# Moving three adjacent groups per partition with two large DMAs, in a group-mean subtraction that is limited by memory traffic

## The chip, the core and the metric

The kernel runs on one core of a Trainium2 chip; the chip's other cores are not used. The metric is device time in microseconds for one execution. One execution was also recorded by the hardware profiler; its page and its trace are what is read here. The engines that matter are DVE (the vector engine, which does all the arithmetic), SP and ACT (whose queues issue the DMAs), and the core's 16 DMA engines, which move data between the chip's memory (HBM) and the core's on-chip memory of 128 partitions.

## The reference

```python
def setup_inputs():
    B, S, D = 8, 4096, 2112
    return {"x": np.random.randn(B, S, D).astype(np.float32)}

def reference(x):
    B, S, D = x.shape
    stride = 4
    x_r = x.reshape(B, S // stride, stride, D)
    pooled = x_r.mean(axis=2)
    upsampled = np.repeat(pooled, stride, axis=1)
    return (x - upsampled).astype(np.float32)
```

Four consecutive rows of 2112 floats form a group. The mean of the group's rows is subtracted from each of them. Input and output are 276.8 MB each. There are 8 x 4096 / 4 = 8192 groups, and a group is one contiguous run of 4 x 2112 x 4 = 33,792 bytes in memory.

## The kernel before

The tensor is seen as 8192 groups of W = 8448 floats, `xg` on the input side and `og` on the output side. One loop takes 128 groups at a time, one to a partition, so it runs 64 times. Below, "a group" in the sense of time means one such pass: 128 partitions with one group each, 4.3 MB in and 4.3 MB out.

In each pass, SP's queue loads the 128 groups into a buffer of the pool `io` (L39), one DMA of 128 rows of 33,792 bytes. The pool has six such buffers. DVE then adds the first two rows into the tile `s` (L43), adds the other two rows to it (L45, twice), and with a single instruction over all four rows (L46) multiplies the sum by -1/4 and adds it to the data in place. ACT's queue stores the buffer (L54), again with a DMA of 128 rows of 33,792 bytes.

There is no schedule written by hand. Each queue works through its own list in program order: SP holds only loads, ACT only stores, DVE only arithmetic. The framework inserts the waits: DVE waits for a load, a store waits for DVE, and a load into a buffer waits until the store that emptied that buffer, six passes earlier, has landed. The tile `s` has one buffer, which only DVE writes and reads. SP and ACT feed the same 16 DMA engines, through one queue each (q1 and q10 on the page).

Of the kernel before, what the change touches and what calls it, by code (L numbers as in the profile page):

```python
# [1 line left out]

# [4 lines left out]

STRIDE = 4
IO_BUFS = 6  # L10


@with_exitstack
def kernel(
    ctx: ExitStack,
    tc: tile.TileContext,
    x: bass.AP,
    out: bass.AP,
):

    nc = tc.nc
    B, S, D = x.shape
    P = nc.NUM_PARTITIONS
    assert S % STRIDE == 0
    G = (B * S) // STRIDE
    W = STRIDE * D

    xg = x.rearrange("b (g f) d -> (b g) (f d)", f=STRIDE)  # L30
    og = out.rearrange("b (g f) d -> (b g) (f d)", f=STRIDE)

    io_pool = ctx.enter_context(tc.tile_pool(name="io", bufs=IO_BUFS))
    sum_pool = ctx.enter_context(tc.tile_pool(name="sum", bufs=1))

    for g0 in range(0, G, P):
        gsz = min(P, G - g0)
        x_tile = io_pool.tile([P, W], mybir.dt.float32)
        nc.sync.dma_start(out=x_tile[:gsz], in_=xg[g0:g0 + gsz])  # L39

        rows = x_tile[:gsz].rearrange("p (f d) -> p f d", f=STRIDE)
        s = sum_pool.tile([P, D], mybir.dt.float32)
        nc.vector.tensor_add(out=s[:gsz], in0=rows[:, 0, :], in1=rows[:, 1, :])  # L43
        for f in range(2, STRIDE):
            nc.vector.tensor_add(out=s[:gsz], in0=s[:gsz], in1=rows[:, f, :])  # L45
        nc.vector.scalar_tensor_tensor(  # L46
            out=rows,
            in0=s[:gsz, None, :].to_broadcast([gsz, STRIDE, D]),
            scalar=-1.0 / STRIDE,
            in1=rows,  # L50
            op0=mybir.AluOpType.mult,
            op1=mybir.AluOpType.add,
        )
        nc.scalar.dma_start(out=og[g0:g0 + gsz], in_=x_tile[:gsz])  # L54


# [1 line left out]
_INS = ['x']  # L58
_OUTS = [((8, 4096, 2112), 'float32')]


# [23 lines left out]
```

## Time and profile before

| | |
|---|---|
| median of 7 runs | 1286.52 us (1286.4 to 1286.9) |
| the profiled execution, its own time | 1286.53 us |
| its span in the profile | 1284.8 us |
| DVE busy | 1026.1 us, 256 instructions |
| bytes moved | 553.70 MB, mean 431 GB/s over the span |
| one load: issue to landing, median | 59.6 us, 64 DMAs of 4224 KB |
| one store: issue to landing, median | 43.8 us, 64 DMAs of 4224 KB |
| one L46 on DVE | 8958 ns, 64 times |
| one L43 or L45 on DVE | 2358 ns, 64 and 128 times |

The time of an execution is a little longer than the span, which runs from the first to the last recorded event of the program. "Issue to landing" is the time from the queue's issue of a DMA to the completion of its last byte; it contains the time that the DMA spends behind others in the queue. A packet is one piece of a DMA as a DMA engine handles it. The share of a queue on the page is the time that its packets took, over the 16 engines' span, and counts only time on the engines.

### The profile page before, as it was taken

To read this page: it belongs to the slowest core of one execution; us is meant where nothing else is said; L and a number is where in the kernel's file an instruction comes from. 1 tells how busy PE (TensorE), PEld (TensorE's weight loads), DVE (VectorE), ACT (ScalarE), POOL (GpSimd) and SP (SyncE) were. 2 spreads that over 40 slices of the span, in tenths; PEclk is the share of its full clock that TensorE was granted. 3 is DMA by queue.
4 is the path that set the end of the run, shared out by engine and by line. 5 is a ranking of instruction groups with operands and counts; after the bars stand their busy time and mean duration, and the time that the engine had idled before them with its cause. 6 is when DMAs were issued, how large, how long until landed. Compare 5 with 4: busy or idle time off the path is not lost.

```text
span 1284.8 us, 674 instructions
## 1 busy us (share of the span) xinstructions
DVE 1026.1 (80%) x256; POOL 0.2 (0%) x4
## 2 busy tenths in 40 slices
DVE  5998778787787877878778787787887878778784
POOL 0000000000000000000000000000000000000000
DMA  9999999999999999999999999999999999999998
GB/s 404 421 438 437 431 428 437 430 437 430 437 430 435 432 436 431 430 436 437 431 429 438 436 428 432 438 433 430 432 437 432 432 431 437 429 433 433 438 429 382
DMA packets 18437, 553.70 MB, mean 431 GB/s; under 512 B 2048, under 2 KB 2048, under 8 KB 2048
## 3 DMA queue, kind: packets, MB, share of 16 engines
q1 hardware_dynamic: 9216, 276.83, 50.0%
q10 hardware_dynamic: 9216, 276.83, 49.9%
q14 instruction: 5, 0.04, 0.0%
HBM read 276.82 MB, written 276.82 MB: 431 GB/s over the span
## 4 chain that ended last, share of the span: by engine, by line
DVE 80%; another core or an unknown queue 17%; DMA 1%; issue 1%; DVEq 0%
DVE x_tile L46 45%; DVE s L45 24%; DVE s L43 12%; DMA x_tile<-in_x_dram 1%; DVEq L43 0%
## 5 line engine op out<-in xcount | busy, mean ns | idle before, releaser
L46 DVE SCALAR_TENSOR_TENSOR x_tile<-s,x_tile 128x8448 f32<-128x8448 f32 x64 | 573.3, 8958 | 2.2
L43 DVE TENSOR_TENSOR s<-x_tile 128x2112 f32<-128x2112 f32 x64 | 150.9, 2358 | 237.5 <-DMA x_tile<-in_x_dram 237.4
L45 DVE TENSOR_TENSOR s<-s,x_tile 128x2112 f32<-128x2112 f32 x128 | 301.8, 2358 | 4.4
L69 POOL MEMSET const-bfloat16-1.0<- 128x1 bf16 x1 | 0.1, 101 | 0.0
L69 POOL MEMSET const-uint8-127<- 128x1 uint8 x1 | 0.1, 101 | 0.0
L69 POOL MEMSET const-float32-0.0<- 128x1 f32 x1 | 0.1, 98 | 0.2 <-issue 0.2
L69 POOL MEMSET const-float32-1.0<- 128x1 f32 x1 | 0.1, 98 | 0.0
## 6 DMA issues: line engine op xcount, KB each, us to landing
x_tile<-in_x_dram SPq DMA_DIRECT2D x64, 4224.0 KB, 59.6
out_dram<-x_tile ACTq DMA_DIRECT2D x64, 4224.0 KB, 43.8
```

What stands on the lines that cost most here:

```text
L43: nc.vector.tensor_add(out=s[:gsz], in0=rows[:, 0, :], in1=rows[:, 1, :])
L45: nc.vector.tensor_add(out=s[:gsz], in0=s[:gsz], in1=rows[:, f, :])
L46: nc.vector.scalar_tensor_tensor(out=rows, in0=s[:gsz, None, :].to_broadcast([gsz, STRIDE, D]), scalar=-1.0 / STRIDE, in1=rows, op0=mybir. ...
L69: nc = _bacc.Bacc("TRN2", target_bir_lowering=False, num_devices=1)
```

## The change

The pool of six buffers becomes one tile, `ring`, of six slots of W floats in each partition: the same size in total. The 64 passes are grouped into blocks: three blocks of one group, nineteen blocks of three groups, four blocks of one group. A block of one is handled as before. In a block of three, each partition owns three adjacent groups of the tensor, a contiguous run of 101,376 bytes in memory and in the ring. This run is moved by two DMAs of 50,688 bytes a partition in each direction. A half therefore holds one and a half groups. DVE still works group by group, with the same four instructions on the same shapes; the middle group of a block needs both halves. The first half is stored after the block's second group, the second half after its third. The three single blocks take slots 0 to 2, the blocks of three take slots 3 to 5 and 0 to 2 in turn, ending in slots 3 to 5, and the last four single blocks take slots 0 to 3.

```diff
-IO_BUFS = 6
+RING = 6
+SUPER = 3
+HEAD = 3
+TAIL = 4
...
-    io_pool = ctx.enter_context(tc.tile_pool(name="io", bufs=IO_BUFS))
+    n = G // P
+    n_super = (n - HEAD - TAIL) // SUPER
+    blocks = [1] * HEAD + [SUPER] * n_super
+    blocks += [1] * (n - sum(blocks))
+
+    ring_pool = ctx.enter_context(tc.tile_pool(name="ring", bufs=1))
     sum_pool = ctx.enter_context(tc.tile_pool(name="sum", bufs=1))
+    ring = ring_pool.tile([P, RING * W], mybir.dt.float32)
 
-    for g0 in range(0, G, P):
-        gsz = min(P, G - g0)
-        x_tile = io_pool.tile([P, W], mybir.dt.float32)
-        nc.sync.dma_start(out=x_tile[:gsz], in_=xg[g0:g0 + gsz])
-
-        rows = x_tile[:gsz].rearrange("p (f d) -> p f d", f=STRIDE)
+    def reduce_group(c0: int):
+        rows = ring[:, c0:c0 + W].rearrange("p (f d) -> p f d", f=STRIDE)
         s = sum_pool.tile([P, D], mybir.dt.float32)
...
-        nc.scalar.dma_start(out=og[g0:g0 + gsz], in_=x_tile[:gsz])
+
+    g0 = 0
+    slot = 0
+    for k in blocks:
+        assert slot + k <= RING
+        src = xg[g0:g0 + k * P].rearrange("(p j) w -> p (j w)", j=k)
+        dst = og[g0:g0 + k * P].rearrange("(p j) w -> p (j w)", j=k)
+        c0 = slot * W
+        parts = 1 if k == 1 else 2
+        step = k * W // parts
+        for h in range(parts):
+            nc.sync.dma_start(
+                out=ring[:, c0 + h * step:c0 + (h + 1) * step],
+                in_=src[:, h * step:(h + 1) * step],
+            )
+        stored = 0
+        for j in range(k):
+            reduce_group(c0 + j * W)
+            while stored < parts and (stored + 1) * step <= (j + 1) * W:
+                nc.scalar.dma_start(
+                    out=dst[:, stored * step:(stored + 1) * step],
+                    in_=ring[:, c0 + stored * step:c0 + (stored + 1) * step],
+                )
+                stored += 1
+        g0 += k * P
+        slot = (slot + k) % RING
```

More of the change, by code (lines that the diff above doesn't have):

```diff
@@ L25 @@
     P = nc.NUM_PARTITIONS
-    assert S % STRIDE == 0
+    W = STRIDE * D
     G = (B * S) // STRIDE
-    W = STRIDE * D
+    assert S % STRIDE == 0 and G % P == 0 and (SUPER * W) % 2 == 0
     xg = x.rearrange("b (g f) d -> (b g) (f d)", f=STRIDE)
     og = out.rearrange("b (g f) d -> (b g) (f d)", f=STRIDE)
-    io_pool = ctx.enter_context(tc.tile_pool(name="io", bufs=IO_BUFS))
-    sum_pool = ctx.enter_context(tc.tile_pool(name="sum", bufs=1))
-    for g0 in range(0, G, P):
-        gsz = min(P, G - g0)
-        x_tile = io_pool.tile([P, W], mybir.dt.float32)
-        nc.sync.dma_start(out=x_tile[:gsz], in_=xg[g0:g0 + gsz])
-        rows = x_tile[:gsz].rearrange("p (f d) -> p f d", f=STRIDE)
+    n = G // P
[3 more added lines that the diff above has]
+    ring_pool = ctx.enter_context(tc.tile_pool(name="ring", bufs=1))
+    sum_pool = ctx.enter_context(tc.tile_pool(name="sum", bufs=1))
+    ring = ring_pool.tile([P, RING * W], mybir.dt.float32)
+    def reduce_group(c0: int):
+        rows = ring[:, c0:c0 + W].rearrange("p (f d) -> p f d", f=STRIDE)
         s = sum_pool.tile([P, D], mybir.dt.float32)
-        nc.vector.tensor_add(out=s[:gsz], in0=rows[:, 0, :], in1=rows[:, 1, :])
+        nc.vector.tensor_add(out=s, in0=rows[:, 0, :], in1=rows[:, 1, :])
         for f in range(2, STRIDE):
-            nc.vector.tensor_add(out=s[:gsz], in0=s[:gsz], in1=rows[:, f, :])
+            nc.vector.tensor_add(out=s, in0=s, in1=rows[:, f, :])
         nc.vector.scalar_tensor_tensor(
             out=rows,
-            in0=s[:gsz, None, :].to_broadcast([gsz, STRIDE, D]),
+            in0=s[:, None, :].to_broadcast([P, STRIDE, D]),
             scalar=-1.0 / STRIDE,
```

## The prediction

> **What bounds the kernel now.** I read the page first, then the busy time by stretch, then the waits, then the timeline of single groups. From the page:
>
> ```profile
> span 1284.8 us, 674 instructions
> DVE 1026.1 (80%) x256; POOL 0.2 (0%) x4
> DMA packets 18437, 553.70 MB, mean 431 GB/s; under 512 B 2048, under 2 KB 2048, under 8 KB 2048
> q1 hardware_dynamic: 9216, 276.83, 50.0%
> q10 hardware_dynamic: 9216, 276.83, 49.9%
> DVE 80%; another core or an unknown queue 17%; DMA 1%; issue 1%; DVEq 0%
> ```
>
> The chain of waits puts 80% on DVE, and that misleads. The two DMA queues together hold the 16 engines for 99.9% of the span. The chain names DVE because it follows each store back to the instruction that released it, while the time is set by how fast the queues drain. Of 18,437 packets, 2048 are completion writes (128 DMAs by 16 engines), a handful are instruction fetches, and 16,384 carry data: 128 a DMA, so one packet for each partition, 33,792 bytes long.
>
> The stretches, with columns of stretch, length, DVE busy, POOL busy, clock, DMA share, GB/s:
>
> ```profile
> 0.00:30.00 30.00, 16.53 (x5) 0.20 (x4) 1.00 0.96 406
> 110.00:1180.00 1070.00, 855.66 (x216) 0.00 (x0) 1.00 1.00 433
> 1255.00:1285.00 30.00, 15.18 (x4) 0.00 (x0) 1.00 0.87 375
> ```
>
> From 110 to 1180 us the DMA engines have no idle time. Only the first and last 30 us have any: 4% and 13%. No reordering of work can win in the middle; only fewer engine-nanoseconds can.
>
> The waits and two groups of the timeline:
>
> ```profile
> DVE s L43 <- DMA x_tile<-in_x_dram: 237.4, 59, 13.3
> SPq L39 <- DMA out_dram<-x_tile: 1158.3, 58, 40.7
> 154.09 2.36 DVE L43 TENSOR_TENSOR s<-x_tile 128x2112 f32<-128x2112 f32 x1 [3.84 <-DMA x_tile<-in_x_dram]
> 174.06 2.36 DVE L43 TENSOR_TENSOR s<-x_tile 128x2112 f32<-128x2112 f32 x1 [3.83 <-DMA x_tile<-in_x_dram]
> ```
>
> DVE starves 3.83 us a group, and the load queue waits for stores to free buffers. One group takes 174.06 - 154.09 = 19.97 us. In that time each engine moves 8 load packets, 8 store packets and 2 completion writes: 19.97 / 16 = 1.248 us a packet.
>
> **The change part by part.** Bytes, the DVE instructions (64 groups of 3 x 2.358 + 8.958 = 16.03 us, 16.17 with the gaps) and the first three and last four groups stay. What moves:
>
> *Fewer packets.* 57 of 64 groups become 19 blocks of three. Each engine did 57 x 16 = 912 data packets for them and now does 19 blocks x 2 DMAs x 2 directions x 8 = 608, of 50,688 bytes: 304 fewer on each engine. Their bytes are not saved, only what a packet costs beyond its bytes. The profile of before has one size of data packet, so this must be bounded. The trace's single packet records show 1251 ns for 16,114 of the 16,384 data packets, 307 to 309 ns for 8192-byte instruction fetches, and 9 ns for the 4-byte completion writes. Lower end: 0, if time is proportional to bytes. Upper end: 9 ns, since a packet with almost no bytes takes no longer than that. Between: the two larger sizes give (1251 - 307) / (33,792 - 8192) = 0.0369 ns a byte and 307 - 8192 x 0.0369 = 4.9 ns left over. I take 4.9, because it comes from large packets. 304 x 4.9 ns = 1.49 us; ends 0 and 2.74 us. A loss is not excluded by these rows; it is priced in the rivals.
>
> The Trainium skill ("DMA: Bandwidth & Descriptors", "Why small descriptors are slow") gives a packet about 3 cycles of fixed cost on the engine's inner bus; with the page's 850 MHz that is an estimate of 3.5 ns, and 304 of them would be 1.1 us. Its section "Anatomy of one DMA" instead gives every DMA about 2 us of fixed cost, and 38 fewer DMAs would then be worth 76 us; the stretch at DMA share 1.00 says that this fixed part lies under other transfers, so the measurement decides against counting it.
>
> *Fewer DMAs.* Each direction goes from 64 to 7 + 38 = 45. That takes 38 completion writes off every engine: 38 x 9 ns = 0.34 us, on the same saturated engines. Issue time on SP and ACT (0.33 us a DMA) lies beside transfers that are tens of microseconds deep, so it is worth nothing; without that cover 19 fewer issues a queue would be 6 us.
>
> *Coarser waits.* A first half covers one and a half groups, and its store can leave only when the second group is done. A half-load waits for the store of the same half two blocks earlier; behind it on SP is only the next load, and ACT has only stores behind its wait. Does the engine queue run dry? A buffer comes round every 6 x 19.97 = 119.8 us. Before: load 20.0 at shared rate, DVE 16.2, store 20.0, and two handovers of 1.4 us (first issue at 0.73, first packet at 1.74, so 1.0; last completion of the first load at 12.95, DVE at 13.33, so 0.4): 59 us, slack 61. After: a half is 6.49 MB; at the shared 433 GB/s its load and its store take 2 x 6.49 / 433 = 30.0 us each. The first half is held for two groups, 32.3 us, or 30.0 + 16.2 = 46.2 if its partner lands a whole half-load later: 95 to 109 us, slack 11 to 25. The second half is held for 32.3 us at most: 95. DVE needs 3 x 16.17 = 48.5 us of each 59.9. So the slack shrinks to between a sixth and two fifths and stays positive: cost 0. What is late next is DVE, which will wait once a block (59.9 - 48.5 = 11.4 us) instead of 3.83 us a group; that costs nothing.
>
> *The end.* The last load now waits for the first half-store of the last block. That block's second group is the 59th pass, which ended at 1254.14 - 5 x 19.97 + 16.17 = 1170 us before and, bunched by up to one pass, at 1190 now. Its store lands 30 us later at the shared rate, 40 with a single store (10 us alone) ahead of it: 1220 to 1230. The load then takes 20.0 at the shared rate and lands at 1240 to 1250, against a last DVE start at 1254.14 before. I take 0. If the two bounds are off by another 7 us together while the final 14.5 us (last store issued at 1270.31, span end 1284.8) stay exposed, up to 3 us is lost. Gain is excluded: the engines have the same bytes to finish.
>
> *The sum.* 1.49 + 0.34 = 1.83 us off. The profiled execution took 1286.53 us (span 1284.8 and 1.7 around it), as good as the median of 1286.52: 1286.53 - 1.83 = 1284.7. With the ends of packet cost (0.34 to 3.08 off) and up to 3 us of exposed end: 1283.4 to 1289.2. About 0.2% (2.6 us) is what a measurement of this kernel can tell from no change, so the forecast is a gain too small to count: no measurable change.
>
> **The rivals.**
>
> *The queue runs dry (slower).* One mechanism: the bunched stores. If slack is used up, both queues of the engines empty once a block, at the wait of a half-load for its half-store (L39's place), and a handover of 1.4 us is bare each time: 19 x 1.4 = 26.6 us, less 1.83: 1311.3. It decides once the hold of a first half exceeds 46.2 + 11 = 57 us. For it: slack falls from 61 to perhaps 11 us. Against: DVE is still 11.4 us a block ahead.
>
> *The new addresses are slower.* Rows are now 101,376 bytes apart instead of adjacent. Nothing in the trace shows a pitch; the nearest rows are the slices of the page, whose full-rate ones range from 428 to 438 GB/s about 433. If the middle runs as the lowest one, 57 x 19.97 x (433 / 428 - 1) = 13.3 us more: 1298.0. Against: nearly every packet record is 1251 ns, read or write, so memory does not show through the engine's rate. The skill's same page ("Latency and other measured facts") has copies slow down at row pitches that are large powers of two; this pitch is none, and no run here shows one.
>
> *A packet's fixed cost is at its upper end (faster).* 9 ns a packet: 2.74 + 0.34 = 3.1 us; with one instruction fetch fewer (0.3 us) as SP and ACT have fewer instructions: 3.4 off, 1283.1. For it: the 9 ns of a completion write. Against: it includes that write's own bytes, and the fetches give 4.9.
>
> *The change does not do what it says.* A 50,688-byte row cut into two packets of 25,344 gives 304 packets more instead of fewer: +1.49 - 0.34, so 1287.7. For it: no packet over 33,792 bytes is in the trace. Worse: if the single ring tile is guarded as a whole, each block's loads wait for all stores before: 30 (two loads alone) + 48.5 + 15 (last half-store alone) + 4 = 97.5 us x 19, and 7 x 39 for the single groups: some 2130 us. Nothing in a profile of before speaks to that, since there every group has a tile of its own.
>
> **How the numbers follow.** Forecast 0.58; fixed cost at its upper end 0.17; cut packets 0.05; dry queue 0.10; slower addresses 0.07; whole-ring guard 0.03. The first three are 0.80; their span sets the range. It begins at 1282.4, a little below 1283.1 for a second fetch saved and a rounding of the 9 ns. It ends at 1288.6: cut packets at 1287.7, and all but the last half microsecond of the exposed end at 1289.2. Faster by over 0.2% is the upper-end case, 0.17; within 0.2% are forecast and cut packets, 0.63; slower is the rest, 0.20.
>
> **What would show it.** Right: 128 x 45 x 2 = 11,520 data packets (608 x 16 = 9728 of them of 50,688 bytes), 1440 completion writes, a DMA share of 1.00 in the middle, DVE idle about 11 us once a block, packet records of 50,688 bytes at 1251 + 16,896 x 0.0369 = 1874 ns. A record near 1867 would mean 9 ns of fixed cost and 1877 none. Wrong: a share under 1.00 in the middle or a drop of GB/s with a period of 60 us (dry queue); records over 1880 ns (addresses); over 20,000 packets (cut); DVE waiting tens of microseconds a block (guard); or an idle stretch just before the last store.

## The result, and the profile after

The changed kernel takes 1320.4 us (median of 12 runs, 1307.0 to 1330.6) against 1286.6 for the kernel before: a ratio of 1.0248, interval 1.0227 to 1.0270. The ratios below leave out runs that were far above the fastest of their kernel, so a ratio and a median of all runs need not agree to the last digit. Two things are new: the loss of 34 us, and the scatter. The kernel before repeats within 0.6 us, the changed one within 24.

From the page of the changed kernel, span and busy time, GB/s in 40 slices, packets, and the two queues (packets, MB, share of 16 engines):

```profile
span 1319.5 us, 527 instructions
DVE 1026.1 (78%) x256; POOL 0.2 (0%) x4
GB/s 418 410 405 438 433 435 433 432 432 430 433 423 439 423 436 439 424 430 432 423 435 424 432 378 432 383 438 398 432 401 435 406 432 406 421 440 348 423 431 323
DMA packets 12964, 553.69 MB, mean 420 GB/s; under 512 B 1440, under 2 KB 1440, under 8 KB 1440
q1 hardware_dynamic: 6480, 276.83, 49.4%
q10 hardware_dynamic: 6480, 276.83, 49.2%
```

The packets are those that were forecast: 11,520 with data, 1440 completion writes. DVE does the same work. The bytes take longer, and they do so increasingly: from the 24th to the 34th slice every other one falls to 378 to 406. Two slices are 66 us, about one block.

The same stretches as before (columns: stretch, length, DVE busy, POOL busy, clock, DMA share, GB/s), the waits of DVE and of the load queue, and the landing times of the blocks' DMAs:

```profile
0.00:30.00 30.00, 16.57 (x5) 0.20 (x4) 1.00 0.96 407
110.00:1180.00 1070.00, 838.61 (x209) 0.00 (x0) 1.00 1.00 425
1180.00:1255.00 75.00, 57.24 (x17) 0.00 (x0) 1.00 0.94 393
1255.00:1320.00 65.00, 39.13 (x9) 0.00 (x0) 1.00 0.86 370
DVE s L52 <- DMA ring<-in_x_dram: 219.1, 19, 14.8
SPq L72 <- DMA out_dram<-ring: 1219.7, 40, 56.5
ring<-in_x_dram SPq DMA_DIRECT2D x38, 6336.0 KB, 42.0
out_dram<-ring ACTq DMA_DIRECT2D x38, 6336.0 KB, 39.5
```

Between 110 and 1180 us the printed share is still 1.00, and yet the engines move 425 GB/s instead of 433: mostly because packets take longer (the packet records show 6.3 us of idle time an engine as well, which the rounded share hides). After 1180 us the engines stand idle for more than that. From the page's rounded shares, the engines' own time is 98.6% of 1319.5 = 1301.0 us, against 99.9% of 1284.8 = 1283.5 before: 17.5 more. Idle is 18.5 against 1.3: 17.2 more. Together these are the 34.7 us of the span.

The single packet records say what the 17.5 is. A 50,688-byte packet takes 1872 ns when nothing disturbs it, but the mean of the loads is 1908 and of the stores 1900, some 20 us more over an engine's 608; the fewer packets take a part of that off again. The longest is 2.2 us too long, and on the load side the long ones are mostly among the first of a DMA. One more thing in the records stood out. A DMA is complete when its last engine has written; the spread from the first of its 16 completion writes to the last was 0.7 us early and at most 2.7 late in the kernel before. In the changed one it is 0.6 for the first load, 3.2 at 117 us, 9.4 at 351 us and at worst 21.1, at 771 us. The 16 engines run apart.

### The profile page after: what moved, and what is told of

It is laid out like the page before. It is cut to its first block, busy times and chain, and to the rows that moved or that the text cites. A ratio compares the mean times of both kernels' runs of the same rounds, so it can differ in the third digit from the quotient of the medians.

```text
span 1319.5 us, 527 instructions
## 1 busy us (share of the span) xinstructions
DVE 1026.1 (78%) x256; POOL 0.2 (0%) x4
## 2 busy tenths in 40 slices
DMA packets 12964, 553.69 MB, mean 420 GB/s; under 512 B 1440, under 2 KB 1440, under 8 KB 1440
## 4 chain that ended last, share of the span: by engine, by line
DMA 60%; DVE 23%; another core or an unknown queue 15%; issue 0%; SPq 0%; DVEq 0%
DMA ring<-in_x_dram 33%; DMA out_dram<-ring 28%; DVE ring L53 14%; DVE s L52 8%; DVE s L50 2%; SPq L72 0%; DVEq L52 0%; DVEq L50 0%
## 5 line engine op out<-in xcount | busy, mean ns | idle before, releaser
L53 DVE SCALAR_TENSOR_TENSOR ring<-s,ring 128x8448 f32<-128x8448 f32 x64 | 573.3, 8958 | 2.2
L52 DVE TENSOR_TENSOR s<-s,ring 128x2112 f32<-128x2112 f32 x128 | 301.9, 2358 | 222.9 <-DMA ring<-in_x_dram 219.1
L50 DVE TENSOR_TENSOR s<-ring 128x2112 f32<-128x2112 f32 x64 | 150.9, 2359 | 56.0 <-DMA ring<-in_x_dram 54.4
## 6 DMA issues: line engine op xcount, KB each, us to landing
out_dram<-ring ACTq DMA_DIRECT2D x38, 6336.0 KB, 39.5
```

Source lines behind the costliest of these rows:

```text
L50: nc.vector.tensor_add(out=s, in0=rows[:, 0, :], in1=rows[:, 1, :])
L52: nc.vector.tensor_add(out=s, in0=s, in1=rows[:, f, :])
L53: nc.vector.scalar_tensor_tensor(out=rows, in0=s[:, None, :].to_broadcast([P, STRIDE, D]), scalar=-1.0 / STRIDE, in1=rows, op0=mybir.AluOp ...
```

## The experiments

Theory S, slack: the coarse, coupled halves leave too little slack for engines that run apart. Rivals: A, the addresses (rows 101,376 bytes apart); P, the 50,688-byte packet by itself.

**e1, thirds.** The addresses alone, with the old DMA size.

```diff
-        parts = 1 if k == 1 else 2
+        parts = 1 if k == 1 else 3
```

> The changed kernel with three DMAs of 33,792 bytes a partition in each block instead of two of 50,688; each third is stored right after its own group. The addresses (three adjacent groups per partition, rows 101,376 bytes apart) and the one ring tile stay. Theory S (slack: the 16 DMA engines drift apart, and the coupled halves leave too little slack to cover the drift): the slack is back at about 61 us a buffer turn, so 1286 to 1288. Theory A (addresses: reads at this pitch collide in memory and make the packets longer): still 1310 to 1325. Theory P (a 50,688-byte packet itself makes the engines drift): 1286 to 1288.

Measured: 1286.45 us, ratio 1.0000 (0.9990 to 1.0009); spread of completion writes at most 2.5 us. The addresses, the single ring tile and the blocks as such cost nothing. Theory A is out.

**e2, four buffers.** The kernel before with less slack.

```diff
-IO_BUFS = 6
+IO_BUFS = 4
```

> The kernel before with four buffers instead of six; nothing else changed. A buffer turn is then 4 x 19.97 = 79.9 us, less 59 of load, DVE, store and handovers: slack 21 us, like the changed kernel's 11 to 25. Theory S: slower, 1295 to 1325, with completion writes of one DMA spread over 10 us or more. Theories A and P: 1286 to 1288, with a spread under 3 us, since addresses and packets are those of before.

Measured: 1290.4, ratio 1.0040 (1.0020 to 1.0059); six of seven executions lie at 1290.2 to 1290.4, one at 1299.6. In the profiled execution, one of the six, the spread stays at 3.8 us or less, and the middle runs at 433 GB/s as before; the 4 us are at the start (30 to 110 us at 421 GB/s instead of 429) and the end. So a computed slack of 21 us, within the range computed for the changed kernel, did no harm in the middle there. Theory S, as an account of slack, missed.

**e3, less work on DVE.**

```diff
-        nc.vector.tensor_add(out=s, in0=rows[:, 0, :], in1=rows[:, 1, :])
-        for f in range(2, STRIDE):
-            nc.vector.tensor_add(out=s, in0=s, in1=rows[:, f, :])
...
+    nc.vector.memset(s, 0.0)   # once, ahead of the loop
```

> The changed kernel with the sums left out: s is zeroed once and each group gets only the one instruction over its four rows (8.96 us instead of 16.17 a group). DMAs, packets, addresses and waits stay. The first half is held 18 us (or 39 if its partner comes a whole half-load later) instead of 32 (46): slack 18 to 39 us instead of 11 to 25. Theory S: most of the loss goes, 1283 to 1300. Theories A and P: nothing changes on the DMA side, 1310 to 1325.

Measured: 1285.9 (1283.9 to 1295.6), ratio 1.0011 (0.9990 to 1.0032). The version leaves out the sums, so it is no replacement. With the same packets and DMAs, a shorter hold gives back practically all, though not the steadiness. Theory P, as a property of the packet alone, cannot stand beside this.

**e4, halves uncoupled.**

```diff
-        for j in range(k):
-            reduce_group(c0 + j * W)
...
+        for h in range(parts):
+            reduce_part(c0 + h * step, step // D)
+            nc.scalar.dma_start(out=dst[:, h * step:(h + 1) * step],
+                                in_=ring[:, c0 + h * step:c0 + (h + 1) * step])
```

> The changed kernel with its halves uncoupled: each half (six rows of a partition) gets its own three additions over its first four rows and one instruction over its six rows, some 20 us, and is stored at once. It leaves out the third group's own mean. Packets of 50,688 bytes, addresses, DMA count, ring and queues stay. A half is held about 21 us: slack 119.8 - 30 - 21 - 30 - 2.8 = 36 us. Theory S: 1282 to 1290, packets at 1872 ns. Theories A and P: 1305 to 1325.

Measured: 1289.8, ratio 1.0028 (1.0016 to 1.0039). The middle runs at 434 GB/s with a spread that stays at 3.8 to 5.1 us for a thousand microseconds. What is lost is at the start (415 GB/s from 30 to 110 us) and at the end. So the engines can be microseconds apart without running further apart; something has to drive them.

**e5, three buffers.** Edit as in e2, with 3.

> The kernel before with three buffers: a turn is 59.9 us, against 59 of load, DVE, store and handovers, so slack of about 1 us, with packets of 33,792 bytes and the old addresses. Theory S (too little slack for the drift between engines): clearly slower, 1310 to 1400, DMA share under 1.00 in the middle, and long first packets of loads as in the changed kernel. Theory C (a coupled pair of 50,688-byte half-loads is needed for the loss, slack alone does not do it): 1290 to 1295, as with four buffers.

Measured: 1338.1, ratio 1.0410 (1.0374 to 1.0446), 418 GB/s in the middle; the stretch, and the stores' landing time:

```profile
110.00:1180.00 1070.00, 831.54 (x208) 0.00 (x0) 1.00 1.00 418
out_dram<-x_tile ACTq DMA_DIRECT2D x64, 4224.0 KB, 22.6
```

Old packets, old addresses, no coupling, and again a loss with the share at 1.00. Theory C is out. One thing differs from the changed kernel: the 16 completion writes of a DMA are at most 6.2 us apart, and under 2 in the median. So a loss of this size does not need engines that run far apart.

**e6 and e7, DVE a little lighter and a little heavier.** One addition less and one more in each group.

```diff
-        for f in range(2, STRIDE):
+        for f in range(2, STRIDE - 1):
```

> The changed kernel with the third addition of each group left out (the mean misses the fourth row): DVE 13.8 us a group instead of 16.2, so the first half is held 4.7 us less and DVE is 7.1 us a block further ahead. Theory S: between the changed kernel and the one with 8.96 us a group, 1288 to 1312, a smaller spread of completion writes. A theory in which DVE does not matter: 1310 to 1325.

> The changed kernel with the fourth row added twice (one addition more in each group): DVE 18.5 us a group, 55.6 a block, still under the 59.8 that a block's bytes need. The first half is held 4.7 us longer. Theory S: slower than the changed kernel, 1325 to 1360. A theory in which DVE does not matter while it is not the bound: 1310 to 1325.

Measured: e6 1298.9, ratio 1.0087 (1.0065 to 1.0109), and the spread creeps from 0.5 to 13 us in its profiled execution, the fastest of four (1293.1); e7 1322.0 (1306.6 to 1334.0), ratio 1.0190 (1.0151 to 1.0229). The lighter side fits. The heavier side does not: the four executions of e7 spread as widely as those of the changed kernel and cannot be told from them.

**e8, three loads and two stores in a block.** The load takes `LOAD_PARTS = 3`, the store keeps two.

> The changed kernel with three loads of 33,792 bytes a partition in each block and still two stores of 50,688, sent as before after the second and third group. A group starts when its own third has landed. Slack by the same account: load 20 + two groups apart 36 + store 30 + handovers 2.8 = 89 of 119.8, so 31 us. Theory S: no drift; 152 packets fewer on an engine at 9 ns and 19 completion writes fewer are 1.5 us off, 1284.5 to 1287, unless the bunched end costs 2 to 4 us. Theory P (a 50,688-byte packet itself is at fault): half of the loss, 1295 to 1310.

Measured: 1397.3 (1333.7 to 1419.4). Even the fastest of its four executions is slower than the slowest of the changed kernel, 1330.6, where all theories expected it to be better. Its trace gave the turn in this work. Both queues' rows, with landing times:

```profile
ring<-in_x_dram SPq DMA_DIRECT2D x64, 4224.0 KB, 58.2
out_dram<-ring ACTq DMA_DIRECT2D x38, 6336.0 KB, 42.0
```

While both queues have work, the engines take their packets in turn, whatever their size: from 160 to 180 us they started 97 load packets and 111 store packets, so loads got 3.3 MB and stores 5.6. Stores of 50,688 bytes against loads of 33,792 drain faster than they are made; from 150 to 160 us there were 128 loads and no store at all. (Those 128 loads are 4.3 MB, 433 GB/s: loads alone still run at the full rate.) The Trainium skill ("DMA: Bandwidth & Descriptors", "Queues, rings and completion order") says that an engine goes round its queues packet by packet. The records agree, with a packet here being one row of one partition, where that section expects some 9 to 17 descriptors in one: chained by their times, all 464 pairs of successive rows in the kernel before, from 150 to 190 us, change from load to store or back.

**e9, quarters.** `parts` 4.

> The changed kernel with four DMAs of 25,344 bytes a partition in each block instead of two of 50,688; the coupling remains (a quarter is stored after the first group that completes it). Theory S now reads: what counts is how many DMAs are in flight against one DMA's pitch, because each ring is refilled one DMA at a time; if a ring runs empty, the next first packet pays its latency and the engines fall out of step. A quarter is held some 32 us of 119.8, so 88 us in flight at a pitch of 15 us are 5.9 DMAs (2.5 to 2.9 in the changed kernel, with the same 88 us or fewer). Theory S: no drift, 1286 to 1291 (304 packets more than before at 9 ns are 2.7 us). A theory by bytes in flight or by addresses: 1300 to 1325.

Measured: 1288.8, ratio 1.0017 (1.0007 to 1.0026). As expected: the coupling is harmless with shorter DMAs.

**e10, the kernel before with a busier DVE.**

> The kernel before with the fourth row added twice: DVE 18.5 us a group, under the pitch of 19.97. In flight are (119.8 - 18.5) / 19.97 = 5.1 DMAs. Theory S: 1286 to 1289, a few us at most for the later last store. A theory in which a busier DVE slows the transfers by itself: 1300 or more.

Measured: 1293.1, ratio 1.0039 (1.0022 to 1.0056), in two clusters: 1286.6 to 1286.9 and 1293 to 1296. The profiled execution is one of the first cluster and shows nothing unusual. The median misses the 1286 to 1289 expected by theory S. What makes the second cluster is open.

**e11, pairs.** Three buffers of two passes, one DMA of two rows a partition for each pair.

```diff
+        x_tile = io_pool.tile([P, 2, W], mybir.dt.float32)   # IO_BUFS = 3
+        nc.sync.dma_start(out=x_tile, in_=xp[n])
```

> The kernel before with two passes moved by one DMA: three buffers of two groups, each DMA 128 x 2 packets of 33,792 bytes at the old addresses, the store after both groups. Ring size, packet size, packet count and alternation are those of before; only DMAs are half as many and twice as long. Held 32.3 of 119.8 us: (119.8 - 32.3) / 39.9 = 2.2 DMAs in flight. Theory S: slower like three single buffers, 1300 to 1345, with rings empty and gaps. Theory P (size of a packet): 1286 to 1292.

Measured: 1332.4, ratio 1.0334 (1.0284 to 1.0385). Same bytes in the ring, same packets and addresses as before, only longer DMAs, stored after both groups: a loss is there again. As in e5 the spread stays small, at most 9.6 us.

```profile
out_dram<-x_tile ACTq DMA_DIRECT2D x32, 8448.0 KB, 45.0
```

**e12, two loads and three stores in a block.** The reverse of e8.

> The changed kernel with two loads of 50,688 bytes a partition in each block and three stores of 33,792. In the opposite case (three loads, two stores) an engine took load and store packets in turn whatever their size, so loads got 40% of the bytes while both queues had work. Here loads get 60%: they run ahead, their ring empties while stores pile up. Theory S with packet turns: slower than before, 1300 to 1400. Without any effect of the turns: 1285 to 1290, by the packets saved.

Measured: 1287.6, ratio 1.0010 (1.0000 to 1.0019). The expectation missed, and usefully so:

```profile
out_dram<-ring ACTq DMA_DIRECT2D x64, 4224.0 KB, 55.0
ring<-in_x_dram SPq DMA_DIRECT2D x38, 6336.0 KB, 34.3
110.00:1180.00 1070.00, 861.41 (x216) 0.00 (x0) 1.00 1.00 434
```

Loads are favoured, so the load queue does run dry: in 17% of the 5 us stretches of the middle over three quarters of the packets are stores. It costs nothing. The stores wait 55 us for their turn and always give the engines something to do. In e8 the queue that ran dry was above all that of the stores. I therefore counted, for the profiled execution of each run, the 5 us stretches from 110 to 1180 us in which at most a quarter of the data packets are stores (the times are those of the profiled executions):

| run | stretches short of stores | time of that execution, us |
|---|---|---|
| before, e1, e2, e3, e4, e10, e12 | 0% | 1283.9 to 1290.4 |
| e9 | 1% | 1288.8 |
| e6 | 4% | 1293.1 |
| changed kernel | 7% | 1321.6 |
| e11 | 7% | 1333.8 |
| e7 | 9% | 1328.7 |
| e5 | 12% | 1337.6 |
| e8 | 34% | 1419.4 |

The small entries mean little: with the stretches shifted by 2.5 us, e6 has under 1%, e3 3% and the changed kernel 9%. That suggested theory Q: it is the store queue that must not run dry. Theory N: any shortage of DMAs in flight. The next pair was to tell them apart at the changed kernel's own packets, addresses and waits, by nothing but the issuing queue.

**e13 and e16, one more queue for loads, or for stores.**

```diff
-            nc.sync.dma_start(
+            (nc.sync if h == 0 else nc.gpsimd).dma_start(        # e13
...
-                nc.scalar.dma_start(
+                (nc.scalar if stored == 0 else nc.gpsimd).dma_start(   # e16
```

> The changed kernel, with only the issuing queue of the second half-load moved from SP to GpSimd. Packets, addresses, coupling and waits stay. If engines take queues in turn by packet, two load queues against one store queue give loads up to two thirds of the packets, so stores wait in line and their queue stays full. Theory Q (the store queue must not run dry, since an engine that has written all its stores waits for the slowest engine's load and for DVE): most of the loss goes, 1283 to 1295, no stretch with under a quarter of stores. Theory N (too few DMAs in flight, whichever queue): no better, 1305 to 1330.

> The changed kernel, with only the issuing queue of the second half-store moved from ACT to GpSimd: two store queues against one load queue. Theory Q: stores leave sooner and their queues run dry more, loads get as little as a third of the packets: slower than the changed kernel, 1325 to 1420. Theory N: as the changed kernel, 1305 to 1330.

Measured: e13 1288.1 (1286.3 to 1288.9), ratio 1.0009 (1.0000 to 1.0018); e16 1327.1 (1325.4 to 1329.6), ratio 1.0317 (1.0303 to 1.0331). The queue rows, the middle stretch and the stores' landing time, first of e13, then of e16 (q0 is GpSimd's queue):

```profile
q10 hardware_dynamic: 6480, 276.83, 49.7%
q1 hardware_dynamic: 3744, 153.55, 27.7%
q0 software_dynamic: 2736, 123.27, 22.2%
110.00:1180.00 1070.00, 868.61 (x219) 8.97 (x17) 1.00 1.00 434
out_dram<-ring ACTq DMA_DIRECT2D x38, 6336.0 KB, 38.4
```

```profile
q1 hardware_dynamic: 6480, 276.83, 49.8%
q10 hardware_dynamic: 3744, 153.55, 26.9%
q0 software_dynamic: 2736, 123.27, 22.2%
110.00:1180.00 1070.00, 834.75 (x209) 9.70 (x18) 1.00 1.00 425
out_dram<-ring ACTq DMA_DIRECT2D x19, 6336.0 KB, 39.6
out_dram<-ring POOLq DMA_DIRECT2D x19, 6336.0 KB, 41.1
```

Favouring the loads lifts the middle from 425 to 434 GB/s and takes 32 us off; favouring the stores leaves it at 425. Stretches short of stores are 1% in e13, 24% in e16. e13 puts theory N out. e16 lies in the ranges of both theories and, with 1325.4 to 1329.6, inside those of the changed kernel, so it does not tell them apart. Nor does e13 work by a shorter hold: from the landing of a first half to the issue of its store it has a median of 49.8 us, the changed kernel 44.6. Nor do loads of the changed kernel wait behind others on SP: each half-load is issued within 0.8 us of the landing of the store that frees its place. So the loss hangs on how the loads queue at the engines, and their share of the turns is the reading that fits e8 and e12 too.

That an empty store queue is where the time goes is shown only in part. For it: chained by their times, the records of the changed kernel show an engine falling idle 80 times in the middle, 6.3 us an engine in all, and in 69 of these a store is what ends the wait. Against it: its stretches short of stores move 430 GB/s, the rest 424, so most of its long packets lie elsewhere; in e5, e8 and e11 the short stretches are the slower ones (387 to 392 GB/s, the rest 406 to 427). The count marks runs that lose, and orders them only roughly: e16 has more short stretches than e5 and loses less.

**e14 and e15, the e12 version with six and nine single blocks at the start.**

> Two loads of 50,688 and three stores of 33,792 bytes a partition in a block (as in e12), and six single blocks at the start instead of three. In e12 the middle ran at 434 GB/s against 433 before, and 30 to 110 us at 418 against 429: some 2 us lost where the blocks begin before the stores have queued up. Both theories on queues: 1285 to 1287, a little under before (18 blocks x 8 packets x 9 ns = 1.3 us and 18 completion writes = 0.2 us saved). If the loss at the start is not from the blocks' early begin: 1287.5.

> As e14 with nine single blocks at the start, so that the blocks begin in the steady state with both queues deep. 17 blocks: 1.2 us of packets saved. 1285 to 1286.5 if the start was the loss, 1287.5 if not.

Measured: 1288.0, ratio 1.0011 (1.0002 to 1.0020), and 1288.4, ratio 1.0016 (1.0007 to 1.0025). The start of e14 is indeed nearly as before (427 GB/s from 30 to 110 us, 429 before), but the time is not less: the loss moves along with the first block (of the 40 slices of GB/s, a low one of 408 to 411 is the third in e12, the fifth in e14 and the seventh in e15). It is the change from single groups to blocks that costs, wherever it stands.

**e17, the e13 version with both ends rearranged.** The first block's second half stays on SP; the second and fourth of the last single loads go to GpSimd.

> As the changed kernel with the second half-loads on GpSimd's queue (e13), but the first block's second half stays on SP, so that it no longer competes with the first single loads, and of the last four single loads the second and fourth go over GpSimd, so that they land earlier. Theory Q: middle as in e13, 1 to 3 us less at the ends: 1284.5 to 1287.5. If the ends are not what is left: 1288.

Measured: 1289.3, ratio 1.0024 (1.0014 to 1.0034). No gain. No version in this study that does the whole work beats the kernel before.

**e18, three buffers with loads on two queues.**

```diff
-        nc.sync.dma_start(
+        (nc.sync if (g0 // P) % 2 == 0 else nc.gpsimd).dma_start(   # IO_BUFS = 3
```

> The kernel before with three buffers (1338), every other load issued from GpSimd instead of SP. Two DMAs are in flight; if the turns let loads land sooner, the rest of the time is spent by stores in their queue. Theory Q: better than 1338, 1295 to 1325, though with so little in flight not all of it. If only the number of DMAs in flight counts here: 1330 to 1345.

Measured: 1377.6, ratio 1.0711 (1.0697 to 1.0726), worse than e5 by 40 us. A clear miss, and a limit of the cure. Two loads are seldom in flight at once here (each lands 23 us after its issue, and one is due every 1378 / 64 = 21.5), so there is no second turn to be had; the share of stretches short of stores rises to 18%. Neither theory expected it: 1295 to 1325 by Q, 1330 to 1345 otherwise. What the second queue adds of its own was not separated.

## Why the prediction was wrong

**The step that failed is "coarser waits", costed at 0.** It asked whether "the engine queue" runs dry and answered with a buffer turn: 95 to 109 of 119.8 us used, 11 to 25 left, so no loss. The runs showed a loss of 33.9 us with slack on paper, which goes away, but for some 3 us at most, with shorter DMAs (e1, e9), with uncoupled halves (e4), with a lighter DVE (e3), and with nothing but a second queue for loads (e13). Three things in that step were wrong. First, it took the two queues as one pool, in which either may be empty as long as the other has work. The runs show that the two are not alike: e12 and e13, where loads get more of the turns, lose nothing in the middle, though e12 is short of loads in 17% of the stretches, while the runs that are most often short of stores (e5, e8, e16, e18) all lose. Second, it took 16 engines as one. A DMA has landed when its last engine has, at worst 21 us after the first one in the changed kernel, and that lag comes off the slack. That such a spread feeds itself is an argument, which no run isolates, and e5 and e11 lose more with spreads under 7 and 10 us. Third, slack was counted in microseconds of a buffer, while each queue is refilled one whole DMA at a time. e9 and e11 show this side: with the same bytes in the ring, short DMAs are harmless and long ones are not. Landing time over the DMA's pitch counts the DMAs in flight: stores had 43.8 / 19.97 = 2.2 before, 39.5 / 29.95 = 1.3 after and 1.1 in e5 and e11. But it is no rule: e13 has 38.4 / 29.95 = 1.3 too, and no loss in the middle.

**The rival that came true was the dry queue,** given 0.10, priced at 1311.3. Its place was right, the load's wait for the half-store. Of its two signs one was seen, the drop of GB/s about once a block; the share in the middle stayed at 1.00. Its condition was wrong: it was to decide above a hold of 57 us, and the first halves were held 44.6 us (median), the second 30.4. Its price, 26.6 us of bare handovers, is near the span's 34.7 by luck: idle time is 17.2 of it, and the other half is long packets, which the rival did not have.

**The term of the packets was right and is real.** Undisturbed records are 940, 1251 and 1872 ns for 25,344, 33,792 and 50,688 bytes, which by the last two would be 9 ns a packet, the upper bound. (The prediction's sign for 9 ns, a record near 1867, was a slip: 9 + 50,688 x (1251 - 9) / 33,792 = 1872.) But each record overlaps the next by some 4 ns, so the pitch decides. In the undisturbed stretches the first completion write of the loads comes every 14.995, 19.965 and 29.903 us (e9, e1, e4): a block takes 59.98 us in quarters, 59.895 in thirds and 59.806 in halves. From one to the next, 16 data packets and 2 completion writes go, and 0.087 us. That is 4.3 to 4.8 ns a packet, on 4.9 forecast, and 19 x 0.087 = 1.7 us a run, on 1.83. The saving is swamped, not absent. Six of the ten executions of e3 lie below every one of the kernel before, at 1283.9 to 1286.0; its shorter DVE work at the end may be a part of that. The saving is also all there is to be had: the ends of e12 to e17 cost more than that. The prediction sets 2 us of fixed cost a DMA aside; the section of the Trainium skill that it names for them ("DMA: Bandwidth & Descriptors", "Anatomy of one DMA") gives them for DMAs issued by GpSimd, and those of this kernel come from SP and ACT.

**Right:** the packet counts; a DVE that waits mainly once a block (219.1 us in 19 waits, 11.5 each, on 11.4 forecast); that neither the addresses nor the tracking of one ring tile costs anything (e1); that a half is one packet. The end was costed at 0 to 3 us; the stretches after 1180 us, with shares of 0.94 and 0.86, hold 4.5 us of idle time and 8.6 up to the span's end; before, the last 30 us held 3.9. So some 9 of the 17.2 lie there. The engines arrive there up to 14 us apart, so I take most of it for the same cause; no run separated it.

**What stays open.** How too few turns for the loads become lost time was seen but not taken apart. The records show loads that take up to 2 us longer at the start of a DMA, stores that take longer as well, and idle gaps where an engine has neither. What sets the first spread in motion, between 100 and 300 us, is not known; nor the two clusters of e10.

## What to carry to other kernels

When loads and stores share saturated DMA engines, look at each queue by itself: landing time over pitch is the number of DMAs it holds, and for stores a value near 1 is a reason to look closer (1.1 to 1.4 in the runs that lost, though 1.3 in e13 did no harm). Packets took turns one for one here, so packet sizes and the number of queues set who gets the bandwidth. Favouring the loads, whose surplus ends up as waiting stores, cured this kernel (e12, e13); favouring the stores did not (e8, e16). It is no general cure: with three buffers a second load queue cost 40 us (e18). Bigger DMAs buy a few nanoseconds a packet with coarser refills, so check the refills first.

## What was unexpected of the hardware

- Turns between queues go by packet and not by byte: 97 load packets of 33,792 bytes against 111 store packets of 50,688 in the same 20 us. A second queue for the same kind of work changes the outcome by 32 us in 1320 (e13).
- The 16 engines do not stay together: completion writes of one DMA came up to 21 us apart in the changed kernel, 2.7 before, with nothing in the program that treats the engines differently.
- How steady the undisturbed engines are: the pitch of 29.903 us in e4 repeats to a nanosecond from block to block for most of the run, with engines 4 to 5 us apart, so distance between engines alone is no instability.
